# Moving 56 transposes of one kernel from TensorE to VectorE and DRAM, and spacing 48 loads evenly

## Chip, core and metric

One core of a Trainium2 chip runs the whole program. The metric is device time in microseconds of one execution, the median of three runs. A profile of one further execution gives the rows below.

## What is computed

Two blocks of two layers each, batch 1, 256 tokens, width 1024, in float32. The first block is a gated delta rule (layer A) and a causal attention with gates (layer B). The second block, with adaptive norms, is a retention (layer C) and a chunked attention over 16 heads (layer D). Cut to the places that matter here:

```
x = x + gated_deltanet(rms_norm(x))                      # A
s = q k^T * scale + bias;  p = softmax(causal s)         # B, 8 heads of 128
x = x + ((p v) * silu(z)) @ w_out                        # B
mod = silu(c) @ ada_w[i] + ada_b[i]                      # for C and for D: shift, scale, gate
o = rms_norm(retention(q, k, v)) * gn_g * silu(g)        # C, 4 heads, values 512 wide
x = x + gate * (o @ w_out)                               # C
x = x + gate * ((softmax(q k^T * scale + bias) v) * silu(g)) @ w_out   # D, 16 heads
```

## The kernel before

Activations live transposed, features on partitions and 256 tokens along the free dimension. A weight matrix is cut into units of 128x1024 floats (512 KB). The task `unit` loads one into one of five `raw` buffers; then ScalarE rounds it to fp32r (`whi`) and VectorE subtracts (`wlo`), into one of six pairs. A projection multiplies a unit in three passes, hi by hi, hi by lo and lo by hi: `project_b` with the weights stationary and 256 columns, `project_a` with the activations stationary and 512 columns. The matrices `in_a_*` to `in_d_*` belong to layers A to D.

The 48 units of `in_ada` hold the adaptive-norm matrices. They go through the same `raw` ring, but one VectorE operation multiplies a unit with the row of `c` and sums it into a column of `mod`; TensorE has no part in it. `_plan` lists all units in the order in which they are loaded and weaves the `ada` units in: 2 late in layer A, 22 from `("b_k", 3)` on, 24 from `("c_v", 3)` on.

The program's order is made by `Tasks`, a planner in the source: every operation has an engine and a booked cost, each engine takes the ready operation with the best priority, and instructions are put out in that order. Each engine's queue then runs in order. All weight loads and all exchanges stand in SyncE's one queue; a wait there holds everything behind it.

A head of attention (`attend`) runs: scores (two fp32 matmuls into PSUM); the softmax on VectorE and ScalarE into `s`; the transpose of the probabilities into `pT`; and the matmuls of `pT` with the values. In layer B the transpose is three TensorE transposes against `ident` into a PSUM bank of the ring `TT`, copied out by ScalarE. In layer D it is an exchange: VectorE transposes all 32x32 blocks into a buffer `z`, `turn_out` stores that to DRAM (`p_d`), and four loads of `turn_in`, one per 32 partitions, bring the blocks to their places in `pT`, in block order; the matmuls read them back through `blocks`. Layer D's queries and keys go through exchanges of 128x1024 as well (`d_q_d`, `d_k_d`, into `con` and `kr`). The planner books such DMAs on an engine of their own, `DB`, which is SyncE in fact.

In layer C the `gate` of a head multiplies the retention's output `o` (buffer `or`) with the gates, transposes it in eight 128x128 pieces with TensorE into the PSUM bank of ring `MM`, and ScalarE and VectorE make the hi and lo parts (`oT`, buffers `xc` for heads 0 and 1, `oc` for heads 2 and 3), scaled by `gn_g`. `out_tile` then multiplies these with the `c_out` units.

Of the kernel before, what the change touches and what calls it, by code (L numbers as in the profile page):

```python
# [10 lines left out]
F32 = mybir.dt.float32  # L11
# [4 lines left out]
ALU = mybir.AluOpType  # L16
# [4 lines left out]
P = 128  # L21
# [90 lines left out]
def _plan():  # L112

    plan = []

    def add(name, *units):
        plan.extend((name, u) for u in units if (name, u) not in plan)

    for u in ORDER:
        if u[0] == "h":  # L120
            add("a_qkv", 8 + int(u[1]), int(u[1]))
        elif u[0] == "v":
            add("a_qkv", 16 + int(u[1]))
        else:
            add("a_z", *range(4 * int(u[1]), 4 * int(u[1]) + 4))
    add("a_out", *range(8))
    for u in ORDER_B:
        add("b_" + u[0], *range(4 * int(u[1]), 4 * int(u[1]) + 4))
    add("b_out", *range(8))
    for u in ORDER_C:  # L130
        n = 2 if u[0] in "kq" else 4
        add("c_" + u[0], *range(n * int(u[1]), n * int(u[1]) + n))
    add("c_out", *range(16))
    add("d_g", *range(FIRST_D))
    for u in ORDER_D:
        add("d_" + u[0], *range(4 * int(u[1]), 4 * int(u[1]) + 4))
    add("d_out", *range(16))

    def weave(units, after, every):
        at = plan.index(after) + 1  # L140
        for u in units:
            plan.insert(at, ("ada", u))
            at += every + 1

    weave(range(ADA_A), ADA_FROM, 2)
    weave(range(ADA_A, 24), ("b_k", 3), 2 if ADA_A > 8 else 1)
    weave(range(24, 48), ADA2_FROM, ADA2_EVERY)
    return plan

# [8 lines left out]
ADA_FROM = ('a_z', 7)  # L158
ADA2_FROM = ('c_v', 3)

EARLY, BATCH, AHEAD, AHEAD2, FIRST_D, ADA_A, ADA2_EVERY = 1, 1, 1, 2, 3, 2, 1
# [8 lines left out]
LATENCY = {"D": 2.0, "D2": 2.0, "DB": 4.0}  # L170
# [89 lines left out]
def _cost_dma(name, o, a, k):  # L260
    return 0.05 + _free(o) * o.shape[0] * 4 / 340e3

# [114 lines left out]
def body(ctx, tc, a, out):  # L377
# [5 lines left out]
    swap = Engine("DB", nc.sync, lambda *x: 0.45)  # L383
# [36 lines left out]
    SS, TT, OO, SQ4 = Ring(run, []), Ring(run, []), Ring(run, []), Ring(run, [])  # L420
# [703 lines left out]
    def attend(A, kT, qT, bias, vv, o, half):  # L1124
# [17 lines left out]
        if "z" not in A:  # L1142
            ps = yield TT
            yield [pe.transpose(ps[:, i * P:(i + 1) * P], x[:, i * P:(i + 1) * P], ident) for i in range(3)]
            A["s"].put(item)
            pT = yield A["pT"]
            yield s.activation(pT, ps[:, :384], AF.Copy)
            TT.put(ps)
        else:
            z = yield A["z"]  # L1150
            yield v.transpose(blocks(z, 3), x.rearrange("p (m b i) -> p m b i", m=3, b=4))
            A["s"].put(item)
            d = tc.dram_tile([P, 384], F32, name="p_d")
            yield turn_out(z, d)
            A["z"].put(z)
            pT = yield A["pT"]
            yield turn_in(pT, d)
        ps = yield OO
        x = blocks(pT, 3) if "z" in A else pT.rearrange("p (m a i) -> p m a i", m=3, a=4)
# [20 lines left out]
    def layer_b(pool, nx, begun, after):  # L1180
# [3 lines left out]
        A = attend_rings(pool, 3)  # L1184
        K, Q, O = ([buf(f"{n}{h}", [P, T]) for h in range(8)] for n in ("k", "q", "o"))
# [200 lines left out]
    def layer_c(pool, nx, first, sin, nsin, cos, rope_in, after, free):  # L1386
# [12 lines left out]
        F = [buf(f"f{h}", [P, 2]) for h in range(4)]  # L1399
        SH = {n: buf(f"sh_{n}", [P, 2]) for n in ("c_k", "c_q")}  # L1400
# [10 lines left out]
        def norm():  # L1411
# [17 lines left out]
            MM.put(ps)  # L1429
# [88 lines left out]
        def gate(h):  # L1518
            yield made["c_g", 4 * h]
            pss = [(yield PJ), (yield PJ)]  # L1520
            yield from project_a("c_g", h, of(hs), pss, hs_in)
            yield GC
            gs = [(yield GS), (yield GS)]
            for t in range(2):
                yield s.activation(gs[t], pss[t], AF.Silu)
                PJ.put(pss[t])
            yield o_in[h]
            o = O[h]
            for t in range(2):
                yield v.tensor_mul(o[:, t], o[:, t], gs[t])  # L1530
                GS.put(gs[t])
            for i in (0, 2):
                ps = yield MM
                yield [pe.transpose(ps[:, (2 * c + t) * P:(2 * c + t + 1) * P], o[:, t, (i + c) * P:(i + c + 1) * P], ident)
                       for c in range(2) for t in range(2)]
                cs = [(oT(4 * h + i + c), ps[:, c * T:(c + 1) * T], col("gn_g", 4 * h + i + c)) for c in range(2)]
                yield [s.activation(hi, x, AF.Copy, scale=w) for (hi, _), x, w in cs]
                yield [v.scalar_tensor_tensor(out=lo, in0=x, scalar=w, in1=hi.bitcast(F32), op0=ALU.mult, op1=ALU.subtract)
                       for (hi, lo), x, w in cs]
                MM.put(ps)  # L1540
            OR.put(o)
            for i in range(4):
                run.set(oT_in[4 * h + i])

        def out_tile(n):
# [6 lines left out]
            yield from project_b(us, oT, None, ps[:, :T], oT_in)  # L1552
# [21 lines left out]
    def layer_d(pool, nx, first):  # L1574
# [22 lines left out]
        def norm():  # L1597
            yield nx.acc_in
            ps = yield MM
# [151 lines left out]
    def main():  # L1751
# [43 lines left out]
        yield from hand_over(XX, TT)  # L1795
# [39 lines left out]
        yield from hand_over(TT, OO)  # L1835
# [97 lines left out]
```

## Time and profile before

| | us |
|---|---|
| median of three runs (lowest to highest) | 794.45 (792.61 to 796.09) |
| the profiled execution | 794.41 |
| its span, first to last instruction | 792.6 |
| TensorE busy (matmuls) | 777.4 |
| VectorE busy | 581.7 |
| ScalarE busy | 444.4 |

The span is what the trace covers; the 1.8 us between it and the execution's time lie around it. Busy times add up all instructions of an engine. For TensorE, matmuls overlap in the pipeline: a 256-column fp32r matmul shows 0.28 us, but the next one starts 0.12 us later. What a matmul costs is therefore the step from start to start. The name of an instruction is `output<-inputs` by the program's tiles; `bank` is a PSUM bank. Nearly all instructions carry the line of one helper (L218), so rows are told apart by tiles.

### The profile page before, as it was taken

What the parts mean: (1) busy time and instruction counts of PE and PEld (TensorE: products, weight loads), DVE (VectorE), ACT (ScalarE), POOL (GpSimd) and SP (SyncE); (2) the same over time, 40 slices, a digit from 0 to 9 for tenths busy, and PEclk for the clock granted to TensorE, in tenths of its full rate; (3) what the DMA queues carried; (4) which work ended last, traced back from release to release, by engine and by line L of the source; (5) the groups of instructions that cost most, each with busy time, mean ns of one, the idle gap of its engine ahead of it and who ended that gap; (6) DMA issues with size and microseconds to landing.
All of it is one profiled execution on the core that took longest, in us unless ns stands there. A gap on an engine that the chain in (4) does not pass through costs nothing.

```text
span 792.6 us, 13576 instructions
## 1 busy us (share of the span) xinstructions
PE 777.4 (98%) x5005; PEld 700.5 (88%) x5005; DVE 581.7 (73%) x1189; ACT 444.4 (56%) x944; POOL 37.4 (5%) x45
## 2 busy tenths in 40 slices
PE   6999999999999999999999999999999999998998
PEld 5898889989898999998978878999888898888998
DVE  5799999445897878788657888867677587766651
ACT  4886454545655686754346455555557566565540
POOL 0120000010000000000000000000100000000000
PEclk9999999999999999999999999999999999999999
DMA  8536343223769875637647988865789879795740
GB/s 284 187 107 211 130 131 115 69 91 117 265 217 335 279 260 189 224 108 270 188 137 226 331 292 311 280 201 171 257 265 285 267 202 289 221 296 182 220 133 28
DMA packets 63227, 165.83 MB, mean 209 GB/s; under 512 B 15247, under 2 KB 26296, under 8 KB 63160
## 3 DMA queue, kind: packets, MB, share of 16 engines
q1 hardware_dynamic: 62104, 163.90, 63.9%
q10 hardware_dynamic: 1056, 1.06, 0.5%
q8 instruction: 39, 0.64, 0.3%
q14 instruction: 28, 0.23, 0.1%
HBM read 156.54 MB, written 8.40 MB: 208 GB/s over the span
## 4 chain that ended last, share of the span: by engine, by line
PE 94%; DMA 3%; DVE 1%; ACT 1%; issue 1%; SPq 0%; POOL 0%; DVEq 0%; ACTq 0%
PE bank L218 94%; DMA d_k_d<-zd 1%; DMA raw<-in_d_g 1%; DMA raw<-in_a_z 1%; DMA xT<-in_xT 1%; DMA kr<-d_k_d 0%; SPq L218 0%; ACT xn L218 0%; DVE wlo L218 0%; ACT js L218 0%; POOL rs L218 0%; DVE r L218 0%; ACT sq L218 0%; DVE hi L218 0%; ACT r L218 0%
## 5 line engine op out<-in xcount | busy, mean ns | idle before, releaser
L218 ACT ACTIVATE whi<-raw 128x1024 fp32r<-128x1024 f32 x210 | 222.0, 1059 | 211.3 <-PE bank L218 170.0
L218 DVE TENSOR_TENSOR wlo<-raw,whi 128x1024 fp32r<-128x1024 f32 x210 | 255.2, 1221 | 84.4 <-ACT whi L218 83.7
L218 PE MATMUL bank<-whi,hd_hi 128*128 128x512 f32 x192 | 78.0, 406 | 0.0
L218 PE MATMUL bank<-wlo,hd_hi 128*128 128x512 f32 x192 | 75.6, 394 | 0.0
L218 PE MATMUL bank<-whi,hd_lo 128*128 128x512 f32 x192 | 75.6, 394 | 0.0
L218 DVE CUSTOM_DVE_ANT_0 raw<-raw,condb 128x1024 f32<-128x1024 f32 x48 | 58.5, 1220 | 8.6 <-DMA raw<-in_ada 8.6
L218 PE MATMUL bank<-whi,hc_hi 128*128 128x512 f32 x128 | 51.9, 406 | 0.0
L218 PE MATMUL bank<-whi,hc_lo 128*128 128x512 f32 x128 | 50.5, 394 | 0.0
L218 PE MATMUL bank<-wlo,hc_hi 128*128 128x512 f32 x128 | 50.4, 394 | 0.0
L218 PE MATMUL bank<-lo,raw 128*128 128x256 f32 x192 | 44.3, 379 | 0.9 <-DVE lo L218 0.9
L218 PEld LDWEIGHTS bank<-whi,hd_lo 128*128 128x128 f32 x192 | 36.1, 188 | 8.4
L218 PEld LDWEIGHTS bank<-wlo,hd_hi 128*128 128x128 f32 x192 | 36.1, 188 | 7.7
L218 PEld LDWEIGHTS bank<-whi,hd_hi 128*128 128x128 f32 x192 | 36.1, 188 | 7.7
L218 PEld LDWEIGHTS bank<-lo,raw 128*128 128x128 f32 x192 | 35.0, 189 | 5.4 <-DVE lo L218 1.1
L218 PE MATMUL bank<-hb_hi,whi 128*128 128x256 f32 x128 | 38.4, 300 | 0.0
L218 PE MATMUL bank<-hb_hi,wlo 128*128 128x256 f32 x128 | 36.2, 283 | 0.0
L218 PE MATMUL bank<-hb_lo,whi 128*128 128x256 f32 x128 | 36.1, 282 | 0.0
L218 PE MATMUL bank<-hd_hi,whi 128*128 128x256 f32 x104 | 30.9, 297 | 0.0
L218 PE MATMUL bank<-hd_hi,wlo 128*128 128x256 f32 x104 | 30.0, 288 | 0.0
L218 PE MATMUL bank<-hd_lo,whi 128*128 128x256 f32 x104 | 29.9, 288 | 0.0
L218 PE MATMUL bank<-ha_hi,whi 128*128 128x256 f32 (+1 forms) x96 | 29.4, 307 | 0.0
L218 PEld LDWEIGHTS bank<-whi,hc_lo 128*128 128x128 f32 x128 | 24.0, 188 | 5.7
(323 smaller groups left out, 2134.3 us busy)
## 6 DMA issues: line engine op xcount, KB each, us to landing
raw<-in_ada SPq DMA_DIRECT2D x48, 512.0 KB, 4.7
raw<-in_a_qkv SPq DMA_DIRECT2D x23, 512.0 KB, 4.7
raw<-in_c_v SPq DMA_DIRECT2D x16, 512.0 KB, 4.4
raw<-in_c_g SPq DMA_DIRECT2D x16, 512.0 KB, 3.7
raw<-in_c_out SPq DMA_DIRECT2D x16, 512.0 KB, 4.9
raw<-in_d_g SPq DMA_DIRECT2D x16, 512.0 KB, 4.6
raw<-in_d_q SPq DMA_DIRECT2D x16, 512.0 KB, 3.9
raw<-in_d_k SPq DMA_DIRECT2D x16, 512.0 KB, 4.3
```

Source lines behind the costliest of these rows:

```text
L218: return self.key, c, lambda: f(*a, **k), func and func.name
```

## The change

Layer B's attention now takes the same exchange as layer D's: the branch for TensorE transposes in `attend` is gone, and `layer_b` makes two `z` buffers (one new, one from `SQ[1]`). Layer C's `gate` puts a head's output through an exchange of 128x1024 (`o_d`, from buffer `z` to buffer `xt`), splits it from SBUF, and `out_tile` reads the parts in block order. The ring `TT` goes: its PSUM bank is a second one for scores in layer B. Layer C's norm hands its bank to the projections (`PJ`), since `MM` has no transposes any more. `weave` spaces a group of `ada` units evenly between two given units. The planner books exchange DMAs by size (`_cost_swap`) with a latency of 3.2 instead of 4.0; layer D, whose code is the same, is planned with these numbers too.

```diff
-    def weave(units, after, every):
-        at = plan.index(after) + 1
-        for u in units:
-            plan.insert(at, ("ada", u))
-            at += every + 1
-
-    weave(range(ADA_A), ADA_FROM, 2)
-    weave(range(ADA_A, 24), ("b_k", 3), 2 if ADA_A > 8 else 1)
-    weave(range(24, 48), ADA2_FROM, ADA2_EVERY)
+    def weave(units, first, last):
+
+        i, j = plan.index(first), plan.index(last)
+        n = len(units)
+        for x in range(n - 1, -1, -1):
+            plan.insert(i + 1 + round((j - i) * x / n), ("ada", units[x]))
+
+    weave(range(24, 48), *ADA_C)
+    weave(range(ADA_A, 24), *ADA_B)
+    weave(range(ADA_A), *ADA_AA)
...
-ADA_FROM = ('a_z', 7)
-ADA2_FROM = ('c_v', 3)
...
+ADA_AA, ADA_B, ADA_C = (("a_z", 7), ("a_out", 7)), (("b_k", 3), ("b_out", 2)), (("c_k", 7), ("c_out", 6))
...
-LATENCY = {"D": 2.0, "D2": 2.0, "DB": 4.0}
+LATENCY = {"D": 2.0, "D2": 2.0, "DB": 3.2}
...
+def _cost_swap(name, o, a, k):
+    return 0.1 + _free(o) * o.shape[0] * 4 / 250e3
...
-    swap = Engine("DB", nc.sync, lambda *x: 0.45)
+    swap = Engine("DB", nc.sync, _cost_swap)
...
-        if "z" not in A:
-            ps = yield TT
-            yield [pe.transpose(ps[:, i * P:(i + 1) * P], x[:, i * P:(i + 1) * P], ident) for i in range(3)]
-            A["s"].put(item)
-            pT = yield A["pT"]
-            yield s.activation(pT, ps[:, :384], AF.Copy)
-            TT.put(ps)
-        else:
-            z = yield A["z"]
...
+        z = yield A["z"]
+        yield v.transpose(blocks(z, 3), x.rearrange("p (m b i) -> p m b i", m=3, b=4))
+        A["s"].put(item)
+        d = tc.dram_tile([P, 384], F32, name="p_d")
+        yield turn_out(z, d)
+        A["z"].put(z)
+        pT = yield A["pT"]
+        yield turn_in(pT, d)
...
+        (more,) = SQ[1].free
+        A["z"] = Ring(run, [buf("z", [P, 384]), more.rearrange("p a t -> p (a t)")[:, :384]])
...
+        ZX, XT = ring(pool, "z", [P, 1024], 1), ring(pool, "xt", [P, 1024], 1)
...
-            MM.put(ps)
+            PJ.put(ps)
...
-            for i in (0, 2):
-                ps = yield MM
-                yield [pe.transpose(ps[:, (2 * c + t) * P:(2 * c + t + 1) * P], o[:, t, (i + c) * P:(i + c + 1) * P], ident)
-                       for c in range(2) for t in range(2)]
...
+            z = yield ZX
+            for t in range(2):
+                yield v.transpose(blocks(z, 8)[:, t::2], o[:, t].rearrange("p (c b i) -> p c b i", c=4, b=4))
             OR.put(o)
...
+            d = tc.dram_tile([P, 1024], F32, name="o_d")
+            yield turn_out(z, d)
+            ZX.put(z)
+            y = yield XT
+            yield turn_in(y, d)
+            for c in range(4):
+                hi, lo = (p.rearrange("p (a u) -> p a u", a=4) for p in oT(4 * h + c))
+                x, w = y.rearrange("p (a c u) -> p a c u", a=4, c=4)[:, :, c], col("gn_g", 4 * h + c)
+                yield s.activation(hi, x, AF.Copy, scale=w)
+                yield v.scalar_tensor_tensor(out=lo, in0=x, scalar=w, in1=hi.bitcast(F32), op0=ALU.mult, op1=ALU.subtract)
+                run.set(oT_in[4 * h + c])
+            XT.put(y)
...
-            yield from project_b(us, oT, None, ps[:, :T], oT_in)
+            yield from project_b(us, lambda k: [p.rearrange("p (a t i) -> p t a i", a=4, t=2) for p in oT(k)], None,
+                                 ps[:, :T].rearrange("p (t a i) -> p t a i", t=2, a=4), oT_in)
...
-        yield from hand_over(XX, TT)
+        yield from hand_over(XX, SS)
...
-        yield from hand_over(TT, OO)
+        yield from hand_over(SS, OO)
```

Where the planner puts things follows from it. SyncE's queue in layer B, around the first `b_z` load, before (each row a DMA, destination from source; `raw` buffers take 512 KB units):

```order
L218 DMA raw_90<-in_b_q 128x1024
L218 DMA raw_94<-in_ada 128x1024
L218 DMA raw_93<-in_b_q 128x1024
L218 DMA raw_91<-in_ada 128x1024
L218 DMA raw_92<-in_b_z 128x1024
L218 DMA raw_94<-in_ada 128x1024
L218 DMA raw_90<-in_b_z 128x1024
L218 DMA raw_91<-in_ada 128x1024
```

Every weight unit is followed by an `ada` unit. The same place after the change, where `sq_78` is the second `z` buffer:

```order
L218 DMA raw_92<-in_ada 128x1024
L218 DMA p_d<-z 128x384
L218 DMA raw_93<-in_b_z 128x1024
L218 DMA raw_94<-in_ada 128x1024
L218 DMA p_d<-sq_78 128x384
L218 DMA pT_1678<-p_d 32x4x96 x4
L218 DMA raw_92<-in_b_z 128x1024
L218 DMA p_d<-z 128x384
L218 DMA raw_91<-in_ada 128x1024
L218 DMA pT_1679<-p_d 32x4x96 x4
L218 DMA raw_94<-in_b_z 128x1024
```

Each head's store and four return loads now stand between the weight loads, and a head's return stands behind the next head's store.

TensorE in layer B around a `pT` matmul, before (`hb` are the normed activations of queries and gates, `k` and `q` give the second head's scores):

```order
L218 MATMUL bank_88<-k_1682,q_1690 128x128
L218 MATMUL bank_88<-k_1682,q_1690 128x256
L218 MATMUL bank_87<-con,s_1672 128x128 x3
L218 MATMUL bank_83<-hb_hi,whi_101 128x256
L218 MATMUL bank_83<-hb_lo,whi_101 128x256
L218 MATMUL bank_83<-hb_hi,wlo_102 128x256
L218 MATMUL bank_86<-hb_hi,whi_97 128x256
L218 MATMUL bank_86<-hb_lo,whi_97 128x256
L218 MATMUL bank_86<-hb_hi,wlo_98 128x256
L218 MATMUL bank_86<-hb_hi,whi_97 128x256
L218 MATMUL bank_86<-hb_lo,whi_97 128x256
L218 MATMUL bank_86<-hb_hi,wlo_98 128x256
```

and after, at the fifth head's `pT` matmuls, which the seventh head's scores follow:

```order
L218 MATMUL bank_83<-hb_hi,whi_95 128x256
L218 MATMUL bank_83<-hb_lo,whi_95 128x256
L218 MATMUL bank_83<-hb_hi,wlo_96 128x256
L218 MATMUL bank_85<-pT_1678,v_1706 128x256
L218 MATMUL bank_85<-pT_1678,v_1706 128x128
L218 MATMUL bank_87<-k_1687,q_1695 128x128
L218 MATMUL bank_87<-k_1687,q_1695 128x256
```

The transposes `con,s` are gone, and a head's `pT` matmul stands three to four heads of scores behind its own scores.

SyncE's queue in layer D at the seventh and eighth heads that run, before:

```order
L218 DMA p_d<-zd 128x384 x2
L218 DMA raw_94<-in_d_q 128x1024
L218 DMA raw_92<-in_d_k 128x1024
L218 DMA pT_4977<-p_d 32x4x96 x4
L218 DMA raw_90<-in_d_k 128x1024
L218 DMA pT_4978<-p_d 32x4x96 x4
L218 DMA raw_91<-in_d_k 128x1024
```

and after:

```order
L218 DMA p_d<-zd 128x384 x2
L218 DMA raw_91<-in_d_q 128x1024
L218 DMA raw_93<-in_d_q 128x1024
L218 DMA pT_5019<-p_d 32x4x96 x4
L218 DMA raw_90<-in_d_k 128x1024
L218 DMA pT_5020<-p_d 32x4x96 x4
L218 DMA raw_92<-in_d_k 128x1024
```

Here the stores, returns and loads follow each other as before.

## Rows read from the trace of the kernel before

**Rows 1.** Page, busy us (share of the span) and instructions of each engine.
```profile
PE 777.4 (98%) x5005; PEld 700.5 (88%) x5005; DVE 581.7 (73%) x1189; ACT 444.4 (56%) x944; POOL 37.4 (5%) x45
```

**Rows 2.** Groups of matmuls (busy, mean ns), then TensorE's timeline: start us, us, what.
```profile
L218 PE MATMUL bank<-con,or 128*128 128x128 f32 x32 | 4.8, 272 | 0.0
L218 PE MATMUL bank<-con,s 128*128 128x128 f32 x24 | 3.9, 272 | 0.0
...
424.31 0.39 PE L218 MATMUL bank<-whi,hc_lo 128*128 128x512 f32 x1
424.55 0.60 PE L218 MATMUL bank<-con,or 128*128 128x128 f32 x4
...
425.21 0.39 PE L218 MATMUL bank<-wlo,hc_hi 128*128 128x512 f32 x1
...
426.14 0.39 PE L218 MATMUL bank<-whi,hc_lo 128*128 128x512 f32 x1
```

**Rows 3.** Timeline of VectorE and of TensorE in layer B.
```profile
230.83 2.35 DVE L218 TENSOR_TENSOR wlo<-raw,whi 128x1024 fp32r<-128x1024 f32 x2
...
233.38 0.28 PE L218 MATMUL bank<-hk_hi,wlo 128*128 128x256 f32 x1
...
236.23 0.28 PE L218 MATMUL bank<-hk_hi,wlo 128*128 128x256 f32 x1
```

**Rows 4.** TensorE's waits: total us, times, longest; then its timeline behind the longest.
```profile
PE bank L218 <- DMA kr<-d_k_d: 2.5, 1, 2.5
PE bank L218 <- DVE lo L218: 0.9, 1, 0.9
...
719.52 0.89 PE L218 MATMUL bank<-kr,qr 128*128 128x128 f32 x4 [2.48 <-DMA kr<-d_k_d]
```

**Rows 5.** Windows: us, busy of each engine, granted clock, DMA share, GB/s.
```profile
core 0: us, PE busy (x) PEld busy (x) DVE busy (x) ACT busy (x) POOL busy (x), PEclk, DMA share, GB/s
230.00:300.00 70.00, 70.00 (x519) 66.77 (x518) 57.38 (x128) 43.79 (x90) 0.00 (x0) 1.00 0.81 279
570.00:745.00 175.00, 172.52 (x938) 149.67 (x937) 123.49 (x257) 108.37 (x288) 12.08 (x9) 0.99 0.82 249
717.04:719.52 2.48, 0.00 (x1) 0.04 (x1) 0.00 (x0) 1.19 (x3) 0.00 (x0) 1.00 0.94 272
720.60:723.90 3.30, 3.30 (x18) 3.30 (x17) 2.71 (x9) 1.40 (x5) 0.00 (x0) 0.50 0.43 170
```

**Rows 6.** Groups of VectorE's block transposes in layer D: busy us, mean ns.
```profile
L218 DVE STREAM_TRANSPOSE zd<-s 128x384 f32<-128x384 f32 x16 | 9.2, 573 | 0.1
L218 DVE STREAM_TRANSPOSE zd<-xn 128x512 f32<-128x512 f32 x8 | 5.7, 707 | 0.1
```

**Rows 7.** VectorE's timeline: start and end of one softmax in layer B.
```profile
254.79 0.29 DVE L218 CUSTOM_DVE_ANT_0 s<-bank,b_bias 128x128 f32<-128x128 f32 x1 [1.28 <-PE bank L218]
...
257.83 0.55 DVE L218 TENSOR_SCALAR s<-s,sm 128x128 f32<-128x128 f32 x2
```

**Rows 8.** DMA issues: KB each, median us to landing; then all of `p_d`.
```profile
p_d<-zd SPq DMA_DIRECT2D x16, 192.0 KB, 3.4
pT<-p_d SPq DMA_DIRECT2D x64, 48.0 KB, 4.1
...
kr<-d_k_d SPq DMA_DIRECT2D x16, 128.0 KB, 3.9
...
DMA to landing us min/median/max: 1.8/3.7/6.9
```

**Rows 9.** Tile `p_d`, 660.6 to 664.25 us (ns, first and last start), then TensorE's timeline.
```profile
L218 SPq DMA_DIRECT2D pT<-p_d x4: 303/340/377, 660.7 to 663.8; - x4
...
DMA to landing us min/median/max: 3.3/5.4/5.8
...
667.28 0.83 PE L218 MATMUL bank<-pT,vr 128*128 128x256 f32 x4
```

**Rows 10.** The same from 699.4 to 703.2 us.
```profile
L218 SPq DMA_DIRECT2D pT<-p_d x4: 302/303/431, 699.5 to 702.7; - x4
...
DMA to landing us min/median/max: 2.8/4.3/5.3
...
706.66 0.81 PE L218 MATMUL bank<-pT,vr 128*128 128x256 f32 x4
```

More of the change, by code (lines that the diff above doesn't have):

```diff
@@ L157 @@
 ORDER_D = "q1 k1 q0 v1 k0 v0 q2 g1 k2 v2 q3 k3 g0 v3 g2 g3".split()
[L158 to L161 removed]
+ADA_AA, ADA_B, ADA_C = (("a_z", 7), ("a_out", 7)), (("b_k", 3), ("b_out", 2)), (("c_k", 7), ("c_out", 6))
+EARLY, BATCH, AHEAD, AHEAD2, FIRST_D, ADA_A = 1, 1, 1, 2, 3, 2
 RAWS, NPARTS, NKQ, NC, NVT = 5, 6, 3, 2, 2
@@ L419, in body @@
     MM = Ring(run, [halves[:, 0], halves[:, 1]])
-    SS, TT, OO, SQ4 = Ring(run, []), Ring(run, []), Ring(run, []), Ring(run, [])
+    SS, OO, SQ4 = Ring(run, []), Ring(run, []), Ring(run, [])
     def hand_over(src, dst, n=1):
@@ L1141, in attend @@
                for t, sl in enumerate(cut)]
-        if "z" not in A:
-            ps = yield TT
-            yield [pe.transpose(ps[:, i * P:(i + 1) * P], x[:, i * P:(i + 1) * P], ident) for i in range(3)]
-            A["s"].put(item)
-            pT = yield A["pT"]
-            yield s.activation(pT, ps[:, :384], AF.Copy)
-            TT.put(ps)
-        else:
-            z = yield A["z"]
[L1151 to L1157, printed above, removed]
+        z = yield A["z"]
[6 more added lines that the diff above has]
+        yield turn_in(pT, d)
         ps = yield OO
-        x = blocks(pT, 3) if "z" in A else pT.rearrange("p (m a i) -> p m a i", m=3, a=4)
+        x = blocks(pT, 3)
         o2 = ps[:, :T].rearrange("p (m a i) -> p m a i", m=2, a=4)
@@ L1531, in gate @@
                 GS.put(gs[t])
-            for i in (0, 2):
-                ps = yield MM
-                yield [pe.transpose(ps[:, (2 * c + t) * P:(2 * c + t + 1) * P], o[:, t, (i + c) * P:(i + c + 1) * P], ident)
-                       for c in range(2) for t in range(2)]
[L1536 to L1540, printed above, removed]
-            OR.put(o)
-            for i in range(4):
-                run.set(oT_in[4 * h + i])
+            z = yield ZX
+            for t in range(2):
+                yield v.transpose(blocks(z, 8)[:, t::2], o[:, t].rearrange("p (c b i) -> p c b i", c=4, b=4))
+            OR.put(o)
+            d = tc.dram_tile([P, 1024], F32, name="o_d")
[10 more added lines that the diff above has]
+            XT.put(y)
         def out_tile(n):
@@ L1598, in norm @@
             yield nx.acc_in
-            ps = yield MM
+            ps = yield PJ
             yield sums_ops(by_token(ps), [acc[:, 0], acc[:, 1]])
```

## Prediction

> **What bounds the kernel now.** I read the busy times first, then TensorE's waits, then the windows, then single stretches of the timeline. TensorE is busy for 777.4 of 792.6 us, the other engines for 73% at most [rows 1]. A busy share alone proves little, since matmul ends are modelled; but starts follow starts without a hole: four 512-column matmuls start 0.93 us apart in all (0.233 us each) [rows 2], 24 of 256 columns 2.85 us apart (0.119 us each) [rows 3]. In the list of what TensorE waited for after its first matmul, one entry is over 1 us: 2.5 us at 719.52 us, for the load `kr<-d_k_d` of an exchange through DRAM [rows 4]. The same stretch is a hole in the windows, and behind it, from 720.60 to 723.90 us, stands a granted clock of 0.50, that is 1.2 GHz [rows 5]. So the time is TensorE's work, plus that one stall, plus start and end. An edit helps only by taking instructions off TensorE, or that stall; it hurts as soon as TensorE waits for something new.
>
> **The change part by part.** The profiled execution took 794.41 us and the median of the runs is 794.45, so the sum starts from 794.4.
>
> *Transposes off TensorE.* 32 of `con,or` (retention) and 24 of `con,s` (second layer's attention) go [rows 2]. From the start of the matmul ahead of a group of four to the start of the second one behind it there are 0.90 us (424.31 to 425.21) [rows 2]; two 512-column matmuls of 0.233 account for 0.47, so four transposes cost 0.43 us, 0.109 each. 56 x 0.109 = 6.1 us. No wait stands around them, so all of it is on the path: **-6.1**.
>
> *Work added beside it.* Eight VectorE transposes of 128x384 at 573 ns and eight of 128x512 at 707 ns [rows 6] are 10.2 us on an engine that is idle for 27% of the span; SyncE issues 60 more DMAs. They cost nothing while the results land ahead of their matmuls. Where they don't, TensorE waits, so each exchange is weighed by the TensorE work that stands between the matmul that starts it and the one that needs it.
>
> *The eight exchanges in the second layer.* In the new order 15.7 to 17.5 us of TensorE work stand between a head's scores and its `pT` matmul (head 1: 105 matmuls of 256 columns and ten fp32 ones). The chain needs: scores to the end of the softmax, 254.79 to 258.38 = 3.6 us [rows 7], and the transpose, 0.6; then by the same kind of exchange in the last layer a median 3.4 us to land in DRAM, four issues of some 0.4 (as in [rows 9]), and 4.1 us to land back [rows 8], together 13.3. With the longest landing of these transfers, 6.9, in place of 4.1 it is 16.1 [rows 8]. The new SyncE order puts another head's store or a weight load ahead of each return, worth about 1 us. So most heads fit and some can miss by 1 to 1.5 us, the eighth's return standing behind a `b_out` load that waits for a split besides; a delay of one head also moves the later ones. I take **+1.5**, from 0 (every head like the medians) to 6 (two rounds of about 3).
>
> *The four exchanges of the retention.* Only the last head is tight: three `c_out` loads stand ahead of its return, and the last of them waits for a split which waits for a matmul; from there to the first use are 85 matmuls, 9.9 us. A split, an issue, four return issues, a landing (3.9 us for `kr<-d_k_d`, 128 KB like this one [rows 8]) and the two operations that make the operands come to about 9.3. I take **+0.5**, from 0 to 2.
>
> *The last layer.* Nothing in its code changes, but the planner now books a 128x384 exchange with less time: by its formulas 0.9 + 3.2 and 1.2 + 3.2 = 8.5 us, where it was 0.45 + 4 and 1.8 + 4 = 10.25. That moves the `pT` matmuls forward. The eighth head in the order in which they run: 63 matmuls of 512 columns between scores and `pT` where there were 72, so 9 x 0.233 = 2.1 us less, and the SyncE rows around it read the same. In the trace its last return load was issued at 663.8 and landed 3.3 us later, 667.1; its `pT` matmul started at 667.28 [rows 9]. The margin was 0.2, so 2.1 less gives a stall near 1.7 with the seventh head's, shared. The twelfth head: last issue 702.7, landed at 705.5 or later, used at 706.66 [rows 10]: margin 1.2 at most, cut by 2.8 (12 matmuls), of which 0.3 is made up by the eleventh's stall: 1.3. The other fourteen lose 0 to 4.9 us of cover; the first group of four has a better SyncE order (its second store no longer goes out with the first), the rest had 2 us or more. I add 0.5 for these. Sum **+3.5**, from 0 to 8.
>
> *The old stall.* Its cover grows by 1.4 us, and the 1.3 us just taken fall inside the same stretch: 2.7 against 2.5. With the stall goes the half clock, 3.3 us at half speed = 1.65. **-4.1**, from -4.1 to -1.
>
> *Even spreading.* The 46 late units are the same transfers and VectorE operations. In the new SyncE order four fewer stand ahead of the sixth `b_z` load. That helps where weights are tightest: around 230 us a split ended at 232.05 (first of the two that start at 230.83) and its first matmul started at 233.38, 1.3 us [rows 3]. Nobody waited, so it earns nothing by itself. The first layer's order shifts between its matmuls; no cost taken, 1 us either way. The freed PSUM bank likewise: 0.
>
> Sum: 794.4 - 6.1 - 4.1 + 3.5 + 1.5 + 0.5 = **789.7 us**.
>
> The Trainium skill (page "VectorE: DVE Perf Modes", section "Rules for kernel authors") says to transpose 128x128 on TensorE where a PSUM destination is acceptable. By that rule this change would give up the cheapest path and the -6.1 would not be earned: 795.8. The row of 0.109 us per transpose on the engine that sets the time speaks against it here; the same page's section "The three transpose paths" says that VectorE does 32x32 blocks only, which is why the change needs DRAM at all, and that half of the price is what the rivals are about.
>
> **The rivals.**
>
> *All exchanges fit.* Every new margin holds: 794.4 - 6.1 - 4.1 = 784.2, say 784 to 786.5. For it: at the medians every head of the second layer has 2 us to spare. Against it: the two margins under 1.3 us.
>
> *The gain is handed back at the exchanges.* The last layer's needs stay as they are and every cut of 2 us comes through, the old stall keeps 1 us, and the second layer misses twice by 3: 784.2 + 8 + 1 + 6, less what overlaps, 792 to 798. For it: landings reach 6.9 us and the margins were thin. Against it: one stall pays for its neighbours.
>
> *Slower: the second layer runs out of transfer time.* From 230 to 300 us the DMA engines are busy for 0.81 at 279 GB/s [rows 5], 56.7 us for 19.5 MB, 2.9 us per MB. In the last layer 175 us at 0.82 are 143.5 us for 43.6 MB; 16 exchanges of 0.39 MB and 8 of 1.05 MB are 14.7 MB of it, the other 28.9 MB cost 84 us at 2.9, which leaves 4.1 us per MB for exchanges, 1.6 us of all engines for one head. Eight are 12.7 us, four units fewer give 6.1 back: 63.3 of 70, so 0.9. If pieces of 384 bytes cost twice that, weights arrive later than their 1.3 to 4 us of margin allow: some 9 us of waiting, each wait with clock lost behind it (3 in all), with the last layer's 3.5: 784.2 + 15.5 = 799.7. It decides from about 14 us of waits on. The Trainium skill (page "DMA: Bandwidth & Descriptors", section "Specifications") wants pieces of 512 bytes or more for full rate and so points the same way; the landings do not show it, since 48 KB loads of such pieces land in 4.1 us and 128 KB loads of 1 KB pieces in 3.9 [rows 8].
>
> *Slower: the retention's output matmuls read in blocks.* Their 384 matmuls now take the moving operand in runs of 32 elements. At 0.12 us each, a third more would be 15 us, 804. No row has fp32r in blocks; fp32 `pT` operands are read so in the last layer without a longer step.
>
> **How the numbers follow.** The measurement tells 0.5% from no change: 790.5 and 798.4 are the bounds. Forecast, 786.5 to 790.5: 0.34. All fits: 0.20. Handed back: 0.34. Transfer time: 0.08. Blocks: 0.04. Faster 0.54, same 0.34, slower 0.12. The range 784.5 to 797.5 leaves out the best corner, the end of "handed back" and both slow cases.
>
> **What would show it.** `con,or` and `con,s` gone from TensorE and its work shorter by 6 us; no clock of 0.50 near 720; TensorE waiting for `pT<-p_d` by under 2 us at a time in the last layer, mostly at the eighth and twelfth heads, and by 1 to 2 us in the second. Wrong if waits for `wlo` or `whi` appear between 240 and 310 us, if `oc` matmuls step by more than 0.12 us, or if a wait brings the half clock back.

## The result: 2.9% slower

The changed kernel takes 817.5 us in the median of four runs (816.3 to 818.3), the kernel before 794.6: a ratio of 1.029, interval 1.026 to 1.032. Forecast were 789.7 us, 0.6% faster, and a range up to 797.5. The sign was wrong. The profiled execution took 817.0 us with a span of 815.2.

The page of the changed kernel, against [rows 1]: engine, busy us and share of the span, instructions. Then its transfer queue: packets, MB, share of 16 engines' span.

```profile
PE 782.2 (96%) x4949; PEld 700.3 (86%) x4949; DVE 587.6 (72%) x1205; ACT 440.2 (54%) x934; POOL 37.8 (5%) x45
...
q1 hardware_dynamic: 70744, 171.25, 66.6%
```

TensorE has 56 instructions fewer, as foretold (the groups `con,or` and `con,s` of [rows 2] are gone), and it is busy for longer all the same, in part since a matmul at a lower clock counts as busy for longer. The transfers grew from 163.90 MB to 171.25. Where the time went is read from TensorE's waits, against [rows 4] (total us, times, longest):

```profile
PE bank L218 <- DMA pT<-p_d: 5.6, 6, 1.7
PE bank L218 <- ACT oc L218: 4.4, 1, 4.4
PE bank L218 <- DMA kr<-d_k_d: 4.2, 2, 2.5
PE bank L218 <- DVE rk L218: 2.7, 1, 2.7
PE bank L218 <- ACT hd_hi L218: 1.4, 1, 1.4
PE bank L218 <- ACT whi L218: 1.2, 2, 0.7
PE bank L218 <- DVE lo L218: 0.9, 1, 0.9
PE bank L218 <- DVE oc L218: 0.9, 1, 0.9
```

Without `lo`, which is the start in both kernels, that is 20.4 us where there were 2.5. Behind four of the waits stands the half clock (windows of the changed kernel, columns as in [rows 5]):

```profile
460.40:463.60 3.20, 3.20 (x10) 2.73 (x11) 2.53 (x4) 0.00 (x0) 0.00 (x0) 0.52 0.29 69
509.60:514.60 5.00, 4.88 (x21) 4.66 (x22) 2.90 (x5) 2.21 (x5) 0.00 (x0) 0.50 0.67 236
648.00:651.20 3.20, 3.20 (x12) 2.73 (x12) 0.72 (x5) 1.16 (x2) 0.00 (x0) 0.50 0.41 164
743.70:746.40 2.70, 2.70 (x14) 2.70 (x14) 1.51 (x5) 1.86 (x6) 0.00 (x0) 0.50 0.19 70
```

The second to last column is the granted clock: 14.1 us at 1.2 GHz, so 7 us lost, where the kernel before lost 1.65 in one stretch. The waits ahead of them were 2.7, 4.4, 1.8 and 2.5 us. Waits +17.9, clock +5.4 and transposes -6.1 make 17.2 of the 22.6 us between the two profiled executions. Of the other five some 1.3 are a longer step of the output matmuls (shown at E9); no row holds the rest.

For the experiments a coarser measure was more useful: how long TensorE took for each layer. I cut the span at three starts: the first `hb_hi,whi` matmul (second layer), the first `xc_hi,whi` (third layer; the last of these ends it) and the last `od,whi`. The rows are those of the tile's instructions on TensorE: duration ns, then first and last start. Before:

```profile
L218 PE MATMUL bank<-hb_hi,whi x128: 277/283/472, 250.0 to 309.1; 128*128 128x256 f32 x128
...
L218 PE MATMUL bank<-xc_hi,whi x96: 277/281/367, 335.6 to 533.5; 128*128 128x256 f32 x64, 128*128 128x258 f32 x32
...
L218 PE MATMUL bank<-od,whi x128: 277/282/365, 744.7 to 788.8; 128*128 128x256 f32 x128
```

After:

```profile
L218 PE MATMUL bank<-hb_hi,whi x128: 276/282/472, 249.4 to 309.9; 128*128 128x256 f32 x128
...
L218 PE MATMUL bank<-xc_hi,whi x96: 277/286/471, 336.4 to 546.5; 128*128 128x256 f32 x64, 128*128 128x258 f32 x32
...
L218 PE MATMUL bank<-od,whi x128: 277/281/363, 765.9 to 811.1; 128*128 128x256 f32 x128
```

So the second layer took 336.4 - 249.4 = 87.0 us where it was 85.6, the third 210.1 where it was 197.9, the last 264.6 where it was 255.3: +1.4, +12.2 and +9.3, against -1.1, -3.0 and -0.6 in the prediction's terms. The table gives the same three stretches for the kernels of the experiments, each from its one profiled execution, and beside them the median of all runs with its ratio to the kernel before on the same chip.

| kernel | second | third | last | median us | ratio (interval) |
|---|---|---|---|---|---|
| before | 85.6 | 197.9 | 255.3 | 794.6 | |
| changed | 87.0 | 210.1 | 264.6 | 817.5 | 1.029 (1.026 to 1.032) |
| E1 spreading alone | 85.5 | 198.4 | 262.0 | 795.4 | 1.001 (0.998 to 1.004) |
| E2 attention exchange alone | 92.1 | 198.0 | 253.9 | 801.7 | 1.009 (1.006 to 1.012) |
| E3 retention exchange alone | 85.6 | 211.4 | 255.8 | 808.4 | 1.017 (1.012 to 1.022) |
| E4 new price alone | 85.6 | 198.0 | 261.8 | 800.2 | 1.006 (1.003 to 1.008) |
| E5 changed, no spreading | 93.8 | 210.3 | 261.0 | 824.4 | 1.037 (1.032 to 1.041) |
| E6 changed, no attention exchange | 85.6 | 204.4 | 261.4 | 808.2 | 1.017 (1.014 to 1.020) |
| E7 changed, no retention exchange | 87.4 | 204.3 | 266.9 | 810.8 | 1.018 (1.012 to 1.023) |
| E8 changed, old price | 87.9 | 203.5 | 261.1 | 804.8 | 1.013 (1.010 to 1.016) |
| E9 = E3 without transfers | 85.6 | 197.0 | 257.5 | 794.9 | 1.000 (0.998 to 1.003) |
| E10 = E3 with whole rows | 85.6 | 210.6 | 256.5 | 808.0 | 1.017 (1.013 to 1.022) |
| E11 before, price 6.0 | 85.6 | 198.0 | 255.5 | 793.7 | 0.998 (0.995 to 1.001) |
| E12 changed, price 6.0 | 87.9 | 205.3 | 257.2 | 806.2 | 1.015 (1.010 to 1.020) |
| E13 = E2 without transfers | 83.8 | 197.9 | 255.8 | 792.3 | 0.997 (0.995 to 0.999) |
| E14 = E3, GpSimd's queue | 85.6 | 217.8 | 255.7 | 812.8 | 1.021 (1.017 to 1.025) |
| E15 before, GpSimd's queue | 85.6 | 198.0 | 277.7 | 817.0 | 1.027 (1.024 to 1.030) |
| E16 = E8, GpSimd's queue | 88.2 | 210.7 | 277.3 | 831.2 | 1.045 (1.042 to 1.048) |
| E17 = E8, early units | 87.8 | 198.8 | 255.4 | 815.5 | 1.026 (1.023 to 1.030) |
| E18 = E1, early units | 85.5 | 199.8 | 252.3 | 814.9 | 1.024 (1.021 to 1.027) |

The last layer's stretch moves by some us from one execution to another (E1's profiled one took 800.8 us, its median is 795.4), so verdicts on that layer go by the medians.

### The profile page after: what moved, and what is told of

It reads as the page before. It is cut to its first block, busy times and chain, and to the rows that moved or that the text cites. A ratio compares the mean times of both kernels' runs of the same rounds, so it can differ in the third digit from the quotient of the medians.

```text
span 815.2 us, 13554 instructions
## 1 busy us (share of the span) xinstructions
PE 782.2 (96%) x4949; PEld 700.3 (86%) x4949; DVE 587.6 (72%) x1205; ACT 440.2 (54%) x934; POOL 37.8 (5%) x45
## 3 DMA queue, kind: packets, MB, share of 16 engines
q1 hardware_dynamic: 70744, 171.25, 66.6%
## 4 chain that ended last, share of the span: by engine, by line
PE 77%; DMA 13%; DVE 5%; SPq 1%; issue 1%; ACT 1%; POOL 0%; DVEq 0%; ACTq 0%
PE bank L218 77%; DMA raw<-in_ada 4%; DMA d_k_d<-zd 2%; DMA kr<-d_k_d 2%; DVE wlo L218 2%; SPq L218 1%; DVE raw L218 1%; DMA raw<-in_d_g 1%; ACT whi L218 1%; DMA xt<-o_d 1%; DMA o_d<-z 1%; DVE s L218 1%; DMA raw<-in_b_z 1%; DMA raw<-in_b_out 1%; DMA raw<-in_a_z 1%
## 5 line engine op out<-in xcount | busy, mean ns | idle before, releaser
L218 DVE CUSTOM_DVE_ANT_0 raw<-raw,condb 128x1024 f32<-128x1024 f32 x48 | 58.5, 1219 | 26.3 <-DMA raw<-in_ada 26.3
L218 PE MATMUL bank<-oc,whi 128*128 128x256 f32 x128 | 25.3, 296 | 5.3 <-ACT oc L218 4.4
```

Source lines behind the costliest of these rows:

```text
L218: return self.key, c, lambda: f(*a, **k), func and func.name
```

## The experiments

**One part at a time (E1 to E4).** My first theory looked at VectorE. In the changed kernel it stood waiting for adaptive-norm loads for 26.3 us in all, where it was 8.6, and it takes its instructions in order:

```profile
DVE raw L218 <- DMA raw<-in_ada: 26.3, 20, 4.0
```

Theory Q laid the slow-down on this, and so on the spreading; theory X on the exchanges; theory L on the planner's new price. Each of the four kernels takes one group of the diff's lines into the kernel before.

E1 takes the new `weave` and its three calls:

```
+    weave(range(24, 48), *ADA_C)
+    weave(range(ADA_A, 24), *ADA_B)
+    weave(range(ADA_A), *ADA_AA)
```

> The kernel before with only the even spreading of the adaptive-norm units. Theory Q (VectorE's queue): after the change VectorE, which takes its instructions in order, stood 26.3 us waiting for adaptive-norm loads (8.6 before), and what was queued behind them (rk, the last operands of the retention) reached TensorE late; the spreading itself does that, so this kernel takes 799 to 805 us with VectorE waiting over 18 us for these loads and TensorE waiting in the third layer. Theory X (the exchanges): the spreading is harmless without the exchanges that share SyncE's queue and the transfers; 793 to 796 us, VectorE's wait for these loads under 12 us.

No change can be measured. Theory Q fell here, though VectorE waited for these loads for 13.1 us, which is between the two expectations.

E2 takes the block transpose with its exchange for the second layer (`attend`, the second `z` buffer, the PSUM bank):

```
+        yield turn_out(z, d)
...
+        yield turn_in(pT, d)
...
+        A["z"] = Ring(run, [buf("z", [P, 384]), more.rearrange("p a t -> p (a t)")[:, :384]])
```

> The kernel before with only the eight exchanges of the second layer (booked by the planner at the old 4.0 us). 24 transposes less on TensorE are 2.6 us. Theory X: about 3 us of waits for pT come with them as in the whole change, 794 to 797 us. Theory Q: the waits come from VectorE's and SyncE's order under the spreading, so most of the 2.6 is earned: 791 to 793 us. Either way the last layer's waits change by under 1 us.

It cost more than either theory had said: 6.4 us, and with the 2.6 us of transposes that it saves, 9.0. TensorE's waits in E2 from 250 to 340 us:

```profile
PE bank L218 <- ACT q L218: 2.8, 2, 2.4
PE bank L218 <- DVE wlo L218: 2.8, 1, 2.8
PE bank L218 <- DMA pT<-p_d: 0.9, 2, 0.7
```

The result of the exchange itself, `pT`, is the smallest of them. The longest `q` is explained by ScalarE's timeline (start us, us, what, and in brackets the idle time before it):

```profile
288.98 1.06 ACT L218 ACTIVATE whi<-raw 128x1024 fp32r<-128x1024 f32 x1 [3.10 <-DMA raw<-in_b_z]
...
290.82 0.36 ACT L218 ACTIVATE q<-bank 128x256 f32<-128x256 f32 x1
```

ScalarE stood 3.1 us for a weight load, `b_z`, and the copy of `q` out of PSUM, for which TensorE waited 2.4 us, was queued behind it. So it was not the exchange that came late but the weights beside it. They did not land late, though: the `b_z` loads landed in 4.8 to 6.6 us where the kernel before has 4.5 to 6.3, and the one that ScalarE waited for in some 4.5 (issued at 284.44). It went out late. SyncE's queue up to it (start us, us, what), and two of its longest waits from 255 to 295 us:

```profile
279.47 0.45 SPq L218 DMA_DIRECT2D raw<-in_ada  x1
282.44 1.94 SPq L218 DMA_DIRECT2D pT<-p_d  x4
284.44 0.41 SPq L218 DMA_DIRECT2D raw<-in_b_z  x1
```

```profile
SPq L218 <- DVE z L218: 3.9, 3, 2.1
...
SPq L218 <- DMA p_d<-sq: 3.1, 2, 2.4
```

Between two weight loads the queue stood 2.4 us for the store of a head, `p_d`, and issued its return for 1.9. In the kernel before it waits in that stretch mostly for VectorE to free weight buffers (10.7 us for `wlo`, 8.9 for `mod`). So here the trace points at SyncE's queue; whether the buffer of that `b_z` load was free any earlier it does not tell.

E3 takes the retention's exchange (`z` and `xt`, the operands made from `xt`, the reading of `oT` in runs of 32):

```
+            d = tc.dram_tile([P, 1024], F32, name="o_d")
+            yield turn_out(z, d)
...
+            yield turn_in(y, d)
```

> The kernel before with only the four exchanges of the retention's outputs. 32 transposes less are 3.5 us. Theory X: the third and the last head's operands land 13 to 17 us after VectorE has transposed them, and TensorE waits for them once for 4 us or more with a half clock behind it, 796 to 802 us. Theory Q: without the late adaptive-norm loads VectorE reaches its transposes 3 to 5 us earlier, TensorE waits under 1 us in the third layer, 790 to 793 us.

Slower than either theory had said: 13.2 us, all of it in the third layer's stretch (+13.5), where theory X saw 796 to 802 us and one wait. Here weights do land late. E3's chain of work (start us, us, what):

```profile
436.71 8.96 DMA raw<-in_c_v
...
445.77 1.06 ACT whi L218
```

and TensorE:

```profile
447.76 0.39 PE L218 MATMUL bank<-hc_hi,whi 128*128 128x256 f32 x1 [3.40 <-ACT vr L218]
```

A `c_v` load, issued 2 us behind the exchange's four loads, took 9.0 us to land where these loads took 4.4 in the median and 5.2 at most in the kernel before; ScalarE waited for it with `vr` queued behind, and TensorE waited 3.4 us for `vr`. The kernel's other new waits are 3.0 us for `wlo`, 3.4 and 0.8 for `oc`, and 1.4 for `hd_hi`.

E4 takes the price alone:

```
-LATENCY = {"D": 2.0, "D2": 2.0, "DB": 4.0}
+LATENCY = {"D": 2.0, "D2": 2.0, "DB": 3.2}
...
+    swap = Engine("DB", nc.sync, _cost_swap)
```

> The kernel before with only the planner's new price of an exchange (latency 3.2 in place of 4.0 us, issue by size). Theory L (booking): the last layer's matmuls that read pT move forward and wait; of the 8.5 us of waits that the changed kernel has in the last layer at least 5 come with it, less the old stall of 2.5: 796 to 801 us. Theories Q and X: under 2 us of new waits, 792 to 796 us.

Theory L is confirmed, though of the waits for `pT` only 2.1 us came; the larger part is the old stall, which is not gone but there twice:

```profile
PE bank L218 <- DMA kr<-d_k_d: 4.3, 2, 2.5
PE bank L218 <- DMA pT<-p_d: 2.1, 3, 1.0
```

The four parts alone make 0.2 + 6.4 + 13.2 + 4.9 = 24.7 us in medians, where the whole change costs 22.9. That is near, but not a proof, since the parts act on each other (E5 to E8).

**One part undone (E5 to E8).** The same four groups of lines, each taken out of the changed kernel.

> The changed kernel with the adaptive-norm units where they were before; all else of the change stays. Theory Q: the third layer's waits (2.7 us for rk, 5.8 us for oc, 1.4 us for hd_hi, and the half clock behind them, some 13 us in all) go for the most part, 803 to 808 us. Theory X: they stay within 3 us, 813 to 818 us.

> The changed kernel with the second layer's attention transposed on TensorE again. 2.6 us of transposes come back, and 2.7 us of waits for pT go: 816 to 819 us by every theory, unless the second layer's transfers push later ones, then 812 to 815.

> The changed kernel with the retention's outputs transposed on TensorE again: 3.5 us of transposes come back. Theory X: the waits for oc and rk and their half clock go, some 11 us, 808 to 812 us. Theory Q: the late adaptive-norm loads stay and VectorE makes the operands as late, so 814 to 820 us.

> The changed kernel with the planner's old price of an exchange (latency 4.0 us, issue 0.45). Theory L: of the 8.5 us of waits in the last layer, and half a clock for 3 to 6 us behind them, most goes: 807 to 811 us. Theories Q and X: the landings are later than either price books, 814 to 818 us.

E5 is a miss of both theories: without the spreading the change is 7 us slower still, and the second layer takes 93.8 us in place of 87.0. So the spreading, worth nothing alone, is worth 7 us beside the exchanges. Why is not shown: it is not that fewer adaptive-norm loads stand in the second layer, since 9 are issued there in E5 and 10 in the changed kernel. From 420 to 515 us it halves them, 24 to 12, and the third layer takes as long in both (210.3 and 210.1). E6 and E8 beat all their expectations. E6 gave 9 us back, of which the second layer's stretch holds 1.4 and the third's 5.7, though the third layer's code is the same; whether transfers pushed back or the planner's order did that is not shown. E7 gave 7, as theory X had said. E8 gave 13, of which 6.6 lie in the third layer's stretch and 3.5 in the last: in the changed kernel the price also books the second and third layer's exchanges, which E4 does not have.

A part's price depends on its company, and not in one direction: the second layer's exchange costs 6.4 us alone and 9.3 beside the others, the price 4.9 and 12.7, the retention's exchange 13.2 and 6.7.

**Transfers or engines (E9, E10, E13).** E9 and E13 keep VectorE's transposes and the operand work and leave the DRAM round trip out, so the blocks stay unswapped.

E9, against E3 (its two `z` buffers are left out here):

```
-            d = tc.dram_tile([P, 1024], F32, name="o_d")
-            yield turn_out(z, d)
-            ZX.put(z)
-            y = yield XT
-            yield turn_in(y, d)
+            y = z
```

> The kernel before with the retention's exchange, but its transfers left out: VectorE transposes the blocks as in the change, and the operands are made straight from the transposed tile (a part of the computation is left out: the blocks stay unswapped). Theory T (transfers): the 13 us that the retention's exchange costs come from its 16 loads and 4 stores, which land 7 us late and hold back the weight loads beside them; without them only the earned transposes stay, 789 to 793 us, and no wait for oc, vr or wlo in the third layer. Theory V (VectorE and ScalarE order): the added VectorE transposes and the regrouped operand work hold up what is queued behind them; most of the waits stay, 800 to 808 us.

E13 does the same in `attend`, for the second layer only:

```
+        pT = z
+        if not here:
             d = tc.dram_tile([P, 384], F32, name="p_d")
```

> The kernel before with the second layer's exchanges, but their transfers left out: VectorE transposes the blocks, and the matmuls read the transposed tile (the blocks stay unswapped, which leaves out that part of the computation). Theory T (transfers): the 6.4 us that these exchanges cost, and the 2.6 that they should earn, come back: 790 to 794 us. Theory V (VectorE's added transposes and order): 798 us or more.

Both costs go with the transfers: from 808.4 to 794.9 us (between the two expectations, nearer to T's), and from 801.7 to 792.3. E13 earns the 2.6 us of its transposes. E9 earns nothing in the median; its third layer is 0.9 us shorter, not 3.5. A wait of 1.0 us for `oc` is left in it, and the output matmuls, which read their operands in block order, step more widely. Equal stretches inside them at the full clock, of the kernel before and of E9:

```profile
501.00:536.00 35.00, 35.00 (x296) 35.00 (x295) 25.81 (x42) 21.64 (x33) 0.00 (x0) 1.00 0.71 227
```

```profile
500.40:535.40 35.00, 35.00 (x288) 34.98 (x288) 28.15 (x44) 20.97 (x32) 0.00 (x0) 1.00 0.82 267
```

That is 0.118 and 0.122 us for a matmul; 384 of them make some 1.3 us (an estimate from these two rows). E1 and E7, which read in plain order, have 297 and 296 in such a stretch. So the two together are 2.3 of the missing 2.6.

E10 moves the same bytes by the same issues, each load as 32 rows of 4 KB where it was 128 pieces of 1 KB:

```
-            yield turn_in(y, d)
+            yield [swap.dma_start(out=y[32 * b:32 * b + 32], in_=d[32 * b:32 * b + 32]) for b in range(4)]
```

> The kernel before with the retention's exchange, the same bytes, queue and issues, but each load brings 32 whole rows of 4 KB in place of 128 pieces of 1 KB (the blocks stay unswapped, which leaves out that part of the computation). Theory P (pieces): the small pieces are what makes the loads land in 7 us; whole rows land in 4 to 5 us and take a smaller share of the transfer engines, 796 to 802 us. Theory T by bytes alone: 805 to 810 us, loads landing in 6 to 8 us as before.

The time is that of E3, as theory T had it. The loads land a little earlier (page of E3, then of E10: KB each, median us to landing):

```profile
xt<-o_d SPq DMA_DIRECT2D x16, 128.0 KB, 7.3
```

```profile
xt<-o_d SPq DMA_DIRECT2D x16, 128.0 KB, 5.8
```

but the transfer engines are as full. The same window, 425 to 515 us, in the kernel before, in E3 and in E9 (DMA share and GB/s stand last):

```profile
425.00:515.00 90.00, 90.00 (x519) 77.10 (x518) 76.67 (x117) 49.18 (x75) 1.40 (x2) 1.00 0.87 296
```

```profile
425.00:515.00 90.00, 79.41 (x397) 65.88 (x396) 70.09 (x104) 39.95 (x58) 1.39 (x2) 0.94 0.95 310
```

```profile
425.00:515.00 90.00, 88.98 (x498) 76.09 (x497) 79.57 (x126) 49.75 (x76) 1.39 (x2) 1.00 0.86 292
```

This is the sum that the prediction did not make. The kernel before kept the transfer engines busy for 0.87 of the retention's stretch, which leaves 90 x 0.13 = 12 us, or 7 up to the 0.95 that E3 reached. The four exchanges are 4.2 MB. E3's queue was busy for 65.5% of 806.2 us = 528; kernels without new transfers stood at 506 (before, 63.9% of 792.6) to 519 (E1, 64.9% of 799.0). So they need 9 to 22 us of all engines and find 7 to 12.

The sum is loose, and a mean over 90 us hides what happens. Around the first exchange of E3, in which the late `c_v` load falls, the engines are full (this measure can read above 1); the same 16 us in E9:

```profile
430.00:446.00 16.00, 14.36 (x74) 11.98 (x72) 8.63 (x13) 5.85 (x8) 0.00 (x0) 1.00 1.04 322
```

```profile
430.00:446.00 16.00, 16.00 (x80) 13.16 (x80) 13.44 (x19) 8.76 (x13) 0.00 (x0) 1.00 0.90 302
```

Two stretches of E3, while the return loads run, and with weight loads alone:

```profile
436.00:440.00 4.00, 4.00 (x19) 3.24 (x18) 1.71 (x2) 1.06 (x1) 0.00 (x0) 1.00 1.09 175
...
442.00:445.00 3.00, 2.36 (x20) 2.16 (x19) 0.59 (x1) 1.46 (x2) 0.00 (x0) 1.00 1.03 410
```

Full engines moved 175 GB/s with the returns among the loads and 410 without; with pieces of 4 KB (E10, 436 to 440 us) it is 228. The mean of the long stretch does not tell the kernels apart: the changed kernel, with its loads spread, has 0.85 at 269 GB/s from 425 to 515 us, less than the kernel before, and its third layer loses 12.2 us all the same. Around its third exchange, from 497 to 509 us, it has 1.04.

**Price and queue (E11, E12, E14 to E16).** In E11 and E12 only the planner's latency is another, 6.0 in place of 4.0 and of 3.2.

> The kernel before with the planner's latency of an exchange raised from 4.0 to 6.0 us (it measures 4 to 6 in the traces). Theory L: the price moves the pT and kr matmuls of the last layer later, the old stall at kr goes with its half clock, 788 to 793 us. If the other work there is too short to move, 793 to 798 us.

> The changed kernel with the planner's latency of an exchange raised from 3.2 to 6.0 us and its price by size kept. Theory L: nothing waits for pT for over 0.5 us in the last layer, and the kr waits shrink: 798 to 804 us, under the 804.8 us that the old price gave. If transfers late beyond any price set the time: 804 to 810 us.

E11 is no change that can be measured: `kr` waits for 0.2 us only, but `pT` now waits for 1.0 and 0.6 and `vr` for 1.0. E12 is no better than the old price in E8. At 6.0 the price moves waits about, and no longer removes them.

In E14 to E16 exchanges are issued from GpSimd's queue. The edit of E15, and of E16 against E8:

```
-    swap = Engine("DB", nc.sync, lambda *x: 0.45)
+    swap = Engine("DB", nc.gpsimd, lambda *x: 0.45)
```

E14 does so for `o_d` and `xt` alone, through an engine of its own at latency 4.0 and issue 0.45.

> The kernel before with the retention's exchange, its 20 transfers issued from GpSimd's queue in place of SyncE's, booked at the old price. Theory S (SyncE's queue): weight loads no longer stand behind the issues and the wait for the store; the waits for oc, vr and wlo fall under 3 us in all, 792 to 798 us. Theory T (room on the transfer engines): the loads still land in 6 to 7 us and hold back the weights, 803 to 809 us.

> The kernel before, with the last layer's exchanges issued from GpSimd's queue. Theory S: the old stall at kr shrinks, 788 to 793 us. Theory T: 793 to 800 us, the stall stays or moves.

> The changed kernel at the old price, with all exchanges issued from GpSimd's queue. It stands against the 804.8 us of the same kernel on SyncE's queue. Theory S: 785 to 795 us. Theory T: 802 to 810 us.

All three are slower than on SyncE's queue and than both theories had said, E15 by 22 us though it moves nothing new. GpSimd's timeline in E14 (start us, us):

```profile
427.81 0.76 POOL L218 DMA_DIRECT2D o_d<-z  x1 [9.23 <-DVE z L218]
435.67 2.21 POOL L218 DMA_DIRECT2D xt<-o_d  x4 [7.10 <-DMA o_d<-z]
```

One issue takes 0.55 to 0.76 us there, where SyncE takes 0.33 for the same store, and the loads land after 6.7 us in the median, where it was 7.3. The weight loads of E14 no longer stand behind the exchange in their queue and land late even so: up to 7.7 us for `c_v`, 9.9 for `c_g` and 9.2 for `c_out`, where the kernel before has 5.2 at most. So theory S does not account for the retention. For the second layer, where E2's trace speaks for it, the test says little: E16's stretch there is 88.2 us and E8's 87.9, and the other queue has costs of its own.

**Room (E17, E18).** The last pair leaves the exchanges alone and clears traffic away: 14 adaptive-norm units are loaded in the first layer, and the last 24 are spread from the third `b_out` load on.

```
-ADA_AA, ADA_B, ADA_C = (("a_z", 7), ("a_out", 7)), (("b_k", 3), ("b_out", 2)), (("c_k", 7), ("c_out", 6))
+ADA_AA, ADA_B, ADA_C = (("a_z", 7), ("a_out", 1)), (("b_k", 3), ("b_out", 2)), (("b_out", 2), ("c_out", 6))
...
-EARLY, BATCH, AHEAD, AHEAD2, FIRST_D, ADA_A = 1, 1, 1, 2, 3, 2
+EARLY, BATCH, AHEAD, AHEAD2, FIRST_D, ADA_A = 1, 1, 1, 2, 3, 14
```

> The changed kernel at the old price, with 14 adaptive-norm units loaded in the first layer (2 before) and the last 24 spread from the third b_out load on. It stands against the 804.8 us of the same kernel without that. Theory T (room): less traffic beside the same exchanges, so their waits shrink in the second and third layer: 794 to 801 us. If the room is not what counts: 802 to 808 us.

> The kernel before with its adaptive-norm units moved in the same way, without exchanges in the second and third layer. Nothing waits there, so less traffic earns nothing: 793 to 796 us, unless the 14 units cost VectorE's time in the first layer, then 796 to 800.

By the medians both miss: the first layer grew by 16 us in either kernel, probably since VectorE now takes these units ahead of that layer's chain (TensorE waits for `ff` 3.4 us at once, for `r` 4.7 in all). Behind the first layer E17 says in part what it was made for. Its rows, against E8's 203.5 and 261.1:

```profile
L218 PE MATMUL bank<-xc_hi,whi x96: 278/287/477, 352.7 to 551.5; 128*128 128x256 f32 x64, 128*128 128x258 f32 x32
...
L218 PE MATMUL bank<-od,whi x128: 277/282/365, 762.8 to 806.9; 128*128 128x256 f32 x128
```

198.8 and 255.4 us: the same exchanges in a third layer with fewer loads beside them (18 adaptive-norm loads in that stretch, where E8 has 24) cost 0.9 us over the kernel before, not 5.6. The third exchange took 11.7 us from its last block transpose to its last landing where it took 12.8 in E8, and the wait of 2.7 us for `oc` is gone. (One execution each; the last layer's 5.7 is within what it moves by itself.) The medians say the same of the whole: with the units moved, the exchanges cost 0.6 us (E17 less E18), without that 9.4 (E8 less E1). The second layer speaks against it: its stretch is 87.8 us in E17 and 87.9 in E8, though the share of the transfer engines in its first 60 us fell from 0.93 to 0.82. The planner's order changes with the units, so room is the likeliest reason in the third layer, and not the only one possible. No version that does the whole computation is faster than the kernel before by more than the measurement tells.

## Why the prediction was wrong

*The step that failed* is the sentence that the added work costs "nothing while the results land ahead of their matmuls", with each exchange then weighed by its own landing against its own cover. That asks whether the exchange is in time; it does not ask what the exchange does to the others. In the retention its transfers fill the engines, and weight loads land up to twice as late (E3); in the second layer its issues and waits stand in SyncE's queue ahead of weight loads, and these go out late (E2). Either way ScalarE or VectorE, which take their work in order, stand at the split of those weights, and the copy out of PSUM for which TensorE waits is behind them. That the costs go with the transfers is shown (E9, E13); by which of the two ways, only by single traces.

*The retention, +0.5.* It measured 13.2 + 3.5 = 16.7. The transfer time of its 4.2 MB stood nowhere in the sum, though a view of windows gives the share of that stretch. The landing was wrong too: 3.9 us was taken from `kr<-d_k_d` [rows 8] as "128 KB like this one", and 6.4 (changed kernel) and 7.3 (E3) were measured in the median. The longest wait was at the third head, not the last one. Its chain in the changed kernel:

```profile
493.78 6.23 DMA o_d<-z
...
502.45 6.60 DMA xt<-o_d
...
509.16 0.52 ACT oc L218
```

From VectorE's last transpose (493.75) to the landing (509.05) are 15.3 us, of which the way out is 6.2. The sum's 9.3 was made for the last head and held no way out.

*The second layer, +1.5.* It measured 6.4 + 2.6 = 9.0 alone; in the whole change, where the spreading helps, its own stretch lost 1.4 in place of winning 1.1. Undoing it gave 9.3 back (E6), most of it behind that layer.

*The last layer, +3.5 - 4.1.* The waits for `pT` came at about their size (in E4 2.1 us, in the changed kernel's last layer 3.5), but at other heads: the second, the fourth and the eleventh, not the eighth. The old stall did not go. I had set its cover, 1.4 us longer, against a landing that would stay as it was; TensorE waited for it again, 1.8 us in E4, and 2.5 us for one before it. Why these loads come later is not settled. The price measured +4.9 (E4, interval 2.3 to 6.7).

*Even spreading, 0.* Right alone (E1), but for too narrow a reason: I wrote that relief at the weights "earns nothing by itself" as nobody waited there. With the exchanges somebody did (`wlo` in E2), and it was worth 7 us (E5).

*The rivals.* "The second layer runs out of transfer time" named the mechanism and its sign, that weights arrive late and clock is lost behind each wait. It got 0.08 and 799.7 us; it summed one layer only, and a mean over 70 us, where the engines are full for some 12 to 16 us at a time. In that layer itself the `b_z` loads did not land late but went out late (E2). "Read in blocks" was right in sign and far too large: 0.122 us a step for 0.118 (E9), 1.3 us and not 15. The conditions for a wrong forecast came true: a wait brought the half clock back four times, `whi` was waited for at 302.65 us in the changed kernel (0.5 us), and `wlo` in E2.

*The Trainium skill.* The rule of the page "VectorE: DVE Perf Modes", section "Rules for kernel authors", to transpose 128x128 on TensorE, was turned down with the row of 0.109 us. The result is on the rule's side, by a way that the row of 0.109 us does not show. Of the page "DMA: Bandwidth & Descriptors", section "Specifications", which asks for pieces of 512 bytes or more, E10 says nothing for or against (both its sizes are above); that pieces of 4 KB in place of 1 bring nothing in time here is measured.

## What to carry to other kernels

Work that is moved from the busiest engine to transfers is also paid by the transfers and the queue that it shares: before looking at whether each result is in time, ask for some 15 us around each exchange whether the transfer engines are full there (a mean over a long stretch hid it here), and what its issues and waits hold up in their queue. A late weight load reaches the busiest engine by way of whatever is queued behind the instruction that waits for it, so look there for the wait, not at the new tile, and look whether the load landed late or was issued late. And weigh a part of a change in company as well as alone: the spreading was worth nothing or 7 us, the price 5 or 13, the retention's exchange 13 or 7.

## What was not expected of the hardware

The round trip through DRAM of 512 KB takes 13 to 18 us from the last block transpose to the last landing while weights stream beside it (E3 and the changed kernel; 11 to 13 in E17), of which 3 to 7 are the way out and 6.4 to 7.3, in the median, the landing of a load. Pieces of 4 KB for 1 KB brought the landing from 7.3 to 5.8 us and the time nowhere. While such loads run, full transfer engines moved 175 GB/s, with weight loads alone 410 (E3). A DMA issue takes 0.55 to 0.76 us on GpSimd and 0.33 on SyncE; the last layer's 24 exchanges, moved there, cost 22 us.
